# SyncE's transfers in the order as written, and a planner that expects later landings, in a two-layer encoder kernel

## The chip, the cores and the metric

The kernel runs on one NeuronCore of a Trainium2 chip. The core has five instruction queues that run side by side and wait for each other by semaphores: TensorE (PE, matrix products), VectorE (DVE), ScalarE (ACT), GpSimd (POOL) and SyncE (SP), which here does nothing but issue transfers (DMAs). The metric is the device time of one execution in microseconds (us); lower is better. All tensors are float32. Products use a split of each operand into a high and a low part (hi and lo) and three products (hi·hi, hi·lo, lo·hi), so every weight that is loaded has to pass ACT (hi) and POOL or DVE (lo = raw − hi) before PE can use it.

## The reference

Two layers of an encoder over 512 positions of width 1024 (a grid of 8 rows by 64 columns), and a last RMSNorm:

```
for l in range(DEPTH):                       # DEPTH = 2
    x = x + hybrid_mixer(rms_norm(x, norm_mix[l]), ...)      # one input projection, 8 neighbourhood heads
                                                             # and 8 grouped-query heads (2 k/v heads), w_out
    x = x + memory_cross_attention(rms_norm(x), rms_norm(mem), ...)   # 4 heads over 256 memory tokens
    x = x + conv_ffn(rms_norm(x), ...)       # up-projection to 2 x 2816, width-3 convolution over positions,
                                             # silu(gate) * val, down-projection
return rms_norm(x, norm_final)
```

Neighbourhood attention adds a learned bias to its scores and masks columns outside the window; the grouped-query heads normalise q and k per head and rotate them by a 2-D position table.

## The kernel before

The activations stay in SBUF transposed, as eight tiles xT of 128 features by 512 positions. The weights come through in pieces of at most 512 KB: SyncE loads a piece into one of two buffers (`raw`, `N_RAW = 2`), ACT writes the high part (`hi<-raw`, L709), POOL or DVE the low part (`lo<-raw,hi`, L710), and PE multiplies. A load into `raw` must wait until the low part of the piece before the last is written, as the buffer is free only then. A layer runs in this order: input projection in the order of `NA_ORDER` (q0, k0, q1, k1, v0 in two pieces, q2, k2, q3, k3, then four pieces `kv` and four `gq`), woven with the neighbourhood attention of four head pairs; grouped-query attention woven with the output projection and the memory keys and values; memory attention; the feed-forward block in three groups.

Beside the weights SyncE moves: biases (`r<-in_bias`, 2 x 384 KB for a head pair, L1076, used by `tensor_tensor_reduce` on the scores, L1264); parameters; memory tokens, once for their statistics (`t<-in_memT`, L1010, squared by ACT at L1012) and once as operands (L980); the rotary tables (L1334 and L1335, multiplied on POOL at L1337); and copies from SBUF to SBUF that bring rows to other partitions: `double` (L1154, `r<-r`, the two k tiles of a pair) and `straddle` (L1240, five copies, v at block borders).

The order on each engine isn't that of the text. The program is written once, and class `Order` then plans a new order for every engine. Each instruction is a `Step` with a duration from a small table. `lifetimes` and `due` work back from the products to a latest time for each step. `run` plays the program forward: on the engines in `FREE` it takes the step that is ready with the earliest latest time (`choose`), on PE it looks up to 240 products ahead for one whose operands are ready by `SURE` (600 ns) before (`product_next`). A transfer in that play costs `DMA_ISSUE` on SyncE, then lands `DMA_NS` later plus its bytes at `DMA_RATE` (330 bytes per ns, shared); at most eight are on the way (`DMA_MOST`). Sixteen rounds change the due times by the products that came late; each round's order is played twice with drawn latencies (`DMA_SPREAD`) and jitter, and the best order is kept. `tc.add_manual_dep` fixes it. SyncE is one of the engines in `FREE`: its transfers are ordered by need, apart from the first fifteen (`SP_IN_ORDER`).

The steps that the prediction speaks of, in the first layer's input projection (about 10 to 75 us):

- `split_k` and `split_q` (L1128 to L1165): a projection in PSUM is scaled by DVE (L1128, L1133), copied by ACT (L1144, L1163) and the rest subtracted by DVE (L1148, L1165). Only then is its PSUM bank (`mm`, four of them) free for the next product.
- `na_scores`: PE's scores, DVE adds the bias (L1264), ACT takes exponentials (L1270); `na_normalise` scales (L954 on POOL, L1282 on ACT); `na_transpose`: PE transposes (L1292), ACT and DVE split (L947, L948); `na_values`: PE multiplies by v (`mm<-r,r`), ACT and DVE combine (L1316 to L1318).

Of the kernel before, what the change touches and what calls it, by code (L numbers as in the profile page):

```python
# [19 lines left out]
P = 128  # L20
# [178 lines left out]
HAND_OVER = {"PE": 60.0, "ACT": 85.0, "DVE": 60.0, "POOL": 80.0, "SP": 60.0}  # L199
# [13 lines left out]
class Step:  # L213
# [99 lines left out]
class Order:  # L313
# [1 line left out]

    FREE = ("ACT", "DVE", "POOL", "SP")
    ORDERED = FREE + ("PE",)

    def __init__(self, tc, kept):
# [71 lines left out]
    def lifetimes(self):  # L393

        self.chain, self.then, self.previous = [list(v) for v in self.after], {}, {}
        first, users, turn = {}, {}, {}
        for s in self.steps:
            for name in s.names:
                if name not in first:
                    first[name] = s.index  # L400
                    turn.setdefault(s.kind(name), []).append(name)
                users.setdefault(name, []).append(s.index)
        for k in SLOTS:
            for old, new in zip(turn[k], turn[k][1:]):
                self.previous[new] = old
                self.then.setdefault(first[old], []).append(first[new])
        for k in IN_TURN:
            for old, new in zip(turn[k], turn[k][SLOTS[k]:]):
                for u in users[old]:
                    if u < first[new]:  # L410
                        self.chain[u].append(first[new])

    def due(self):

        start, now = {}, FIRST_PRODUCT
        for s in self.steps:
            if s.engine == "PE":
                start[s.index] = now - self.credit.get(s.index, 0.0)
                now += s.busy
        end = now + 1e4  # L420
        self.latest = [end] * len(self.steps)
        for s in reversed(self.steps):
            until = min([end] + [self.latest[j] - self.wait(s, self.steps[j]) for j in self.chain[s.index]])
            if s.engine == "PE":
                self.latest[s.index] = start[s.index]
            elif s.dma:
                self.latest[s.index] = until - DMA_NS - s.bytes / DMA_RATE
            else:
                self.latest[s.index] = min([until - s.takes] + [self.latest[j] for j in self.then.get(s.index, ())])

    def run(self, given=None, draw=None):


# [9 lines left out]
        written = [s.index for s in steps if s.engine == "PE"]  # L443
        at = 0
        open_ = {e: [s.index for s in steps if s.engine == e and not need[s.index]] for e in self.FREE}
        issued, shared = set(), {"DVE": 0.0, "POOL": 0.0}
        order, late, product = {e: [] for e in self.ORDERED}, [], None

        moving, clock, last, gate = [], 0.0, 0.0, 0.0

        def possible(j, ready):

            if need[j] or self.kept.get(j, -1) >= 0 and self.kept[j] not in issued:
                return None
            t, wanted = ready[j], {}
            if steps[j].engine == "SP":

                if len(moving) >= DMA_MOST:
                    return None
                t = max(t, gate)  # L460
# [12 lines left out]
            return t  # L473
# [34 lines left out]

        def product_next():

            mine, i, seen, best = written, at, 0, None
            while i < len(mine) and seen < AHEAD_MOST:
                j = mine[i]
                i += 1
                if j in issued:
                    continue
                seen += 1
                t = earliest(j)
                if t is None:
                    continue  # L520
                sure = max(t, possible(j, fed) + SURE)
                if best is None or sure < best[0] - PATIENCE:
                    best = sure, t, j
                if best[0] <= free_at["PE"] + PATIENCE:
                    break
            return best and best[1:]
# [44 lines left out]
        while len(issued) < n or moving:  # L571
            best = None
            for e in HAND_OVER:
                if e != "PE" or given is not None:
                    c = choose(e)
                else:
                    c = product_next()
                if c and c[0] is not None and (best is None or c[0] < best[0]):
                    best = c
            j = transfers(best[0] if best else 1e18)  # L580
            if j is not None:
                if len(moving) == DMA_MOST - 1:
                    gate = clock
                over_(steps[j], clock, clock)
                continue
            t, j = best
            s = steps[j]
            e = s.engine
            if e in self.FREE:
                open_[e].remove(j)  # L590
            if e in self.ORDERED:
                order[e].append(s)
            if e == "PE":
                short = MARGIN - (t - possible(j, fed))
                if product is not None and short > 0:
                    late.append((j, t - product, t - product + short))
                product = t + s.busy

            if e == "POOL":
                t = max(t, shared["DVE"])  # L600
                if s.wide(s.reads) or getattr(s.ins, "op", None) == ALU.pow:
                    shared["POOL"] = t + s.busy
            elif s.two_from_sbuf():
                t = max(t, shared["POOL"])
                shared["DVE"] = t + s.busy
            slow = 1.0 if draw is None or e in ("PE", "SP") else 1.0 + 0.04 * draw.random()
            free_at[e] = t + s.busy * slow
            issued.add(j)
            while at < len(written) and written[at] in issued:
                at += 1  # L610
# [17 lines left out]
def encoder_kernel(ctx: ExitStack, tc: tile.TileContext, t: dict, out: bass.AP):  # L628
    nc = tc.nc
    kept = set()  # L630
    PE, SP = Counted(nc.tensor), Free(nc.sync)
    SP_IN_ORDER = InOrder(tc, nc.sync, kept)
    late = Late(PE)
    ACT_IN_ORDER = InOrder(tc, nc.scalar, kept)
    ACT, DVE, POOL = Free(nc.scalar), Free(nc.vector), Free(nc.gpsimd)
# [191 lines left out]
    for n in FIRST:  # L827
        if isinstance(n, int):
            if n == 0:
                SP_IN_ORDER.dma_start(x0, t["x0"])  # L830
            else:
                SP_IN_ORDER.dma_start(xT[n], t["xT"][n * P : (n + 1) * P, :])
# [5 lines left out]
        (nc.scalar if n == FIRST[1] else SP_IN_ORDER).dma_start(raw[:, k0:k1], loads[0][1][:, k0:k1])  # L838
# [1066 lines left out]
```

## Time and profile before

| | |
|---|---|
| median of 3 runs | 1337.96 us (1336.49 to 1338.44) |
| the profiled execution's own time | 1337.63 us |
| its span in the profile | 1335.8 us |
| granted PE clock, mean of the span | 0.997 |
| transfers | 136.80 MB, 102 GB/s over the span |

The profile of one execution gives the busy time of each engine, the chain of waits that ended last, who waited for whom, and every instruction with its start. "Idle before" a group of instructions is the time in which the engine stood still, and the releaser behind the arrow is what ended it. A transfer has two times: its issue on SyncE's queue (SPq), and its landing, which is when its reader may start. The busy time of PE is modelled over pipelined products: one of 512 columns is listed with about 0.39 us while the next starts 0.23 us after it, so the gaps are better read from start times.

### The profile page before, as it was taken

Reading aid. Unit: us, or ns where it says so; the run is one execution under the profiler, and the core shown is the slowest. Engines: PE = TensorE matmul, PEld = TensorE weight load, DVE = VectorE, ACT = ScalarE, POOL = GpSimd, SP = SyncE. Lnnn points to the kernel's source line nnn. Section 1 sums busy time; section 2 is a strip of 40 time slices with the busy share of each in tenths; the row PEclk is TensorE's granted clock in tenths of the full one; section 3 lists DMA queues with packets and bytes.
Section 4 is the critical chain, followed back from the end, with each engine's and each line's share of the span. In section 5 each row is a group of like instructions: output and inputs, shape, how many; then the busy total and the mean of one; then the engine's idle time right before and its main releaser. Section 6 shows DMA issues by size and latency. Waiting matters only on the chain.

```text
span 1335.8 us, 18121 instructions
## 1 busy us (share of the span) xinstructions
PE 1326.2 (99%) x6544; PEld 1117.7 (84%) x6544; DVE 885.4 (66%) x1574; ACT 685.0 (51%) x1258; POOL 708.4 (53%) x496
## 2 busy tenths in 40 slices
PE   9999999999999999999999999999999999999998
PEld 8888888888888888888888888888888888888887
DVE  6569875675984388178535697776769825862874
ACT  6668776654442244244446687765544423432434
POOL 2667965636444443444736578664544444444443
PEclk9999999999999999999999999999999999999998
DMA  7753322313333333333356413222233333333321
GB/s 227 201 149 87 110 67 61 110 52 100 101 96 95 95 95 95 104 100 101 98 146 186 143 57 102 64 75 84 64 101 101 99 95 96 91 99 101 102 82 64
DMA packets 203706, 136.80 MB, mean 102 GB/s; under 512 B 5344, under 2 KB 193760, under 8 KB 203616
## 3 DMA queue, kind: packets, MB, share of 16 engines
q1 hardware_dynamic: 202800, 134.98, 34.7%
q8 instruction: 52, 0.85, 0.3%
q10 hardware_dynamic: 816, 0.66, 0.1%
q14 instruction: 38, 0.31, 0.1%
HBM read 125.65 MB, written 2.10 MB: 96 GB/s over the span
## 4 chain that ended last, share of the span: by engine, by line
PE 93%; ACT 2%; DVE 2%; DMA 1%; issue 1%; POOL 0%; SPq 0%; POOLq 0%; ACTq 0%; DVEq 0%
PE mm L95 81%; PE sc L95 7%; PE tr L1447 2%; PE tr L95 1%; PE tr L1292 1%; DMA r<-r 1%; PE tr L1626 1%; ACT t L1270 0%; ACT hi L709 0%; DMA raw<-in_w_in 0%; DVE r L1165 0%; ACT r L1144 0%; DVE sc L1264 0%; ACT r L947 0%; DVE r L948 0%
## 5 line engine op out<-in xcount | busy, mean ns | idle before, releaser
L710 POOL TENSOR_TENSOR lo<-raw,hi 128x512 fp32r<-128x512 f32 (+3 forms) x278 | 528.9, 1913 | 516.1 <-ACT hi L709 474.0
L95 PE MATMUL mm<-xg,hi 128*128 128x512 f32 x1728 | 534.1, 390 | 0.0
L709 ACT CAST hi<-raw 128x512 fp32r<-128x512 f32 (+3 forms) x282 | 232.1, 841 | 335.3 <-PE mm L95 277.1
L95 PEld LDWEIGHTS mm<-xg,hi 128*128 128x128 f32 x1728 | 322.6, 188 | 65.9
L95 PE MATMUL mm<-r,hi 128*128 128x512 f32 (+1 forms) x1200 | 348.7, 371 | 0.1
L95 PE MATMUL mm<-xg,lo 128*128 128x512 f32 x864 | 336.3, 389 | 0.0
L1728 DVE SCALAR_TENSOR_TENSOR t<-t,par,t 128x7 f32<-128x7 f32 (+1 forms) x352 | 245.9, 757 | 25.9 <-ACT t L1721 25.9
L95 PEld LDWEIGHTS mm<-r,hi 128*128 128x128 f32 x1200 | 217.9, 188 | 38.4 <-ACT hi L709 0.6
L95 PE MATMUL mm<-r,lo 128*128 128x512 f32 (+1 forms) x600 | 222.0, 371 | 0.0
L95 PEld LDWEIGHTS mm<-xg,lo 128*128 128x128 f32 x864 | 162.2, 188 | 33.8
L95 PEld LDWEIGHTS mm<-r,lo 128*128 128x128 f32 x600 | 113.0, 188 | 19.2
L95 PE MATMUL mm<-hi,xg 128*128 128x512 f32 (+1 forms) x384 | 110.4, 360 | 1.7 <-DVE r L1148 1.6
L1713 DVE TENSOR_TENSOR t<-mm,rep 128x512 f32<-128x512 f32 x88 | 60.0, 686 | 59.7 <-PE mm L95 44.0
L954 POOL TENSOR_SCALAR t<-t,s 128x512 f32<-128x512 f32 (+1 forms) x112 | 66.7, 611 | 57.7 <-DVE s L1431 33.7
L1757 DVE TENSOR_TENSOR xT<-xT,mm 128x512 f32<-128x512 f32 x32 | 21.9, 686 | 104.5 <-PE mm L95 104.5
L1733 ACT CAST r<-t 128x512 fp32r<-128x512 f32 x44 | 27.3, 620 | 108.9 <-DVE t L1731 108.9
L1731 DVE TENSOR_TENSOR t<-t,t 128x512 f32<-128x512 f32 x44 | 74.3, 1689 | 5.2 <-ACT t L1730 1.2
L95 PEld LDWEIGHTS mm<-hi,xg 128*128 128x128 f32 x384 | 68.1, 189 | 11.1 <-DVE r L1148 1.9
L95 PE MATMUL sc<-r,r 128*128 128x256 f32 (+1 forms) x352 | 74.3, 330 | 0.0
L95 PE MATMUL mm<-lo,xg 128*128 128x512 f32 (+1 forms) x192 | 68.4, 359 | 0.0
L1721 ACT ACTIVATE t<-t,par 128x512 f32<-128x512 f32 x88 | 67.0, 806 | 0.7 <-DVE t L1713 0.7
L1425 ACT ACTIVATE t<-sc,s,qr 128x512 f32<-128x512 f32 x64 | 49.3, 776 | 25.7 <-DVE s L954 25.1
(166 smaller groups left out, 1551.3 us busy)
## 6 DMA issues: line engine op xcount, KB each, us to landing
raw<-in_w_up SPq DMA_DIRECT2D x88, 512.0 KB, 3.8
raw<-in_w_in SPq DMA_DIRECT2D x25, 512.0 KB, 4.1
raw<-in_w_down SPq DMA_DIRECT2D x24, 448.0 KB, 3.6
raw<-in_w_down SPq DMA_DIRECT2D x20, 512.0 KB, 3.9
raw<-in_w_mem_kv SPq DMA_DIRECT2D x16, 512.0 KB, 3.8
r<-in_bias SPq DMA_DIRECT2D x16, 384.0 KB, 4.9
r<-r SPq DMA_DIRECT2D x22, 256.0 KB, 3.5
raw<-in_w_in SPq DMA_DIRECT2D x18, 256.0 KB, 3.9
```

The lines of the kernel that those rows point to most:

```text
L95: return self.engine.matmul(out, lhsT, rhs, **k)
L709: act.copy(hi[:, k], raw[:, k])
L710: (POOL if eng[0] == "P" else DVE).tensor_sub(lo[:, k], raw[:, k], f(hi)[:, k])
L954: eng.tensor_scalar(e, e, sums[:, col : col + 1], 1.0, op0=ALU.mult, op1=ALU.mult)
L1425: ACT.activation(e, sc[j], AF.Exp, bias=nmx[:, c], scale=qrs[b][:, col : col + 1], accum_out=sums[:, c])
L1447: PE.transpose(tr[:, k * P : (k + 1) * P], es[j][:, k * P : (k + 1) * P], ident)
L1713: DVE.tensor_mul(u, us[side], ffn.rep)
L1721: ACT.activation(cc, u, AF.Identity, bias=par[:, l, CB + ch : CB + ch + 1], scale=w[1])
L1728: DVE.scalar_tensor_tensor(cc[:, dst], u[:, src], wi, cc[:, dst], op0=ALU.mult, op1=ALU.add)
L1731: DVE.tensor_mul(cs[0], cs[0], cs[1])
L1733: ACT.copy(acts[j][0], cs[0])
L1757: DVE.tensor_add(xT[m], xT[m], pm)
```

## The change

Two sizes that the planner uses are moved, and one engine is taken out of its hands.

- `DMA_NS` goes from 3000 to 3500, `DMA_SPREAD` from 1900–3100 to 2700–4200, and `SURE` from 600 to 500.
- SyncE is no longer in `FREE`. All its transfers go through `InOrder`, in the order in which the program text issues them. The play takes them from a list (`written["SP"]`), and a transfer waits until the eighth before it in that list has landed (`gate`). The due time of a transfer is now no later than that of the next in the list (`queue`), and `lifetimes` makes a transfer also a forerunner of the one eight places behind it.
- In `possible`, a step may open a buffer only if it is the first in the text to use it.

```diff
-DMA_ISSUE, DMA_NS, DMA_RATE, DMA_SHARE, DMA_GAP, DMA_MOST = 480.0, 3000.0, 330.0, 0.6, 150.0, 8
+DMA_ISSUE, DMA_NS, DMA_RATE, DMA_SHARE, DMA_GAP, DMA_MOST = 480.0, 3500.0, 330.0, 0.6, 150.0, 8
-DMA_SPREAD, JITTER = (1900.0, 3100.0), 200.0
-AHEAD_MOST, PATIENCE, SURE = 240, 60.0, 600.0
+DMA_SPREAD, JITTER = (2700.0, 4200.0), 200.0
+AHEAD_MOST, PATIENCE, SURE = 240, 60.0, 500.0
...
-    FREE = ("ACT", "DVE", "POOL", "SP")
+    FREE = ("ACT", "DVE", "POOL")
...
+        queue = [s.index for s in self.steps if s.dma and s.engine == "SP"]
+        self.gate, self.follows = dict(zip(queue[DMA_MOST:], queue)), dict(zip(queue, queue[DMA_MOST:]))
+        for a, b in self.follows.items():
+            self.chain[a].append(b)
...
-                self.latest[s.index] = until - DMA_NS - s.bytes / DMA_RATE
+                queue = self.latest[s.index] = min(until - DMA_NS - s.bytes / DMA_RATE, queue - s.busy)
...
+            if j in self.gate and self.gate[j] not in landed:
+                return None
...
+                    if self.first[name] != j:
+                        return None
...
-    PE, SP = Counted(nc.tensor), Free(nc.sync)
-    SP_IN_ORDER = InOrder(tc, nc.sync, kept)
+    PE, SP = Counted(nc.tensor), InOrder(tc, nc.sync, kept)
```

No instruction is added or taken away: both programs have 323 transfers on SyncE and the same products. Only the places change. In the built programs 1102 of 6472 products, 291 of 1101 ACT instructions, 329 of 1574 on DVE, 86 of some 490 on POOL and 76 of 323 transfers have another place in their queue. All moved products lie, by their times in the profile before, between 23 and 300 us and between 729 and 954 us; in the feed-forward blocks PE's order is the same. The transfers that move most are those of the first 70 us. After the fifteen first loads SyncE's queue reads (weights by their names in `NA_ORDER`):

```
before: bias0, bias0, par, par, k1, gfin, v0a, memT1, v0b, q2, k2, double1, double1, q3, bias1, bias1,
        straddle x4, k3, straddle, memT2, rope, kv0 x2, qkg, kv1 x2, memT3, double2 x2, kv2 x2, bias2 x2, kv3 x2
after:  k1, v0a, v0b, q2, bias0, bias0, par, par, gfin, k2, q3, k3, double1, double1, memT1, bias1, bias1,
        straddle x5, kv0 x2, memT2, rope, qkg, kv1 x2, kv2 x2, memT3, double2 x2, bias2 x2, kv3 x2
```

On ACT the four exponentials of the second unit (L1270) stood behind the split of kv0 (L709) and now stand ahead of it; on POOL that unit's normalisation (L954) stood behind the low part of kv0 and the first half of the rotary table's product (L1337), and now stands ahead of both. At the end of the kernel two of the six result stores on SyncE change places.

More of the change, by code (lines that the diff above doesn't have):

```diff
@@ L395, in lifetimes @@
         self.chain, self.then, self.previous = [list(v) for v in self.after], {}, {}
-        first, users, turn = {}, {}, {}
+        self.first, users, turn = {}, {}, {}
+        first = self.first
         for s in self.steps:
@@ L420, in due @@
         end = now + 1e4
-        self.latest = [end] * len(self.steps)
+        self.latest, queue = [end] * len(self.steps), end
         for s in reversed(self.steps):
@@ L442, in run @@
                 left[name] = left.get(name, 0) + 1
-        written = [s.index for s in steps if s.engine == "PE"]
-        at = 0
+        written = {e: [s.index for s in steps if s.engine == e] for e in HAND_OVER}
+        at = dict.fromkeys(HAND_OVER, 0)
         open_ = {e: [s.index for s in steps if s.engine == e and not need[s.index]] for e in self.FREE}
-        issued, shared = set(), {"DVE": 0.0, "POOL": 0.0}
+        issued, landed, shared = set(), set(), {"DVE": 0.0, "POOL": 0.0}
         order, late, product = {e: [] for e in self.ORDERED}, [], None
-        moving, clock, last, gate = [], 0.0, 0.0, 0.0
+        moving, clock, last = [], 0.0, 0.0
         def possible(j, ready):
@@ L581, in run @@
             if j is not None:
-                if len(moving) == DMA_MOST - 1:
-                    gate = clock
+                landed.add(j)
+                if j in self.follows:
+                    ready[self.follows[j]] = max(ready[self.follows[j]], clock)
                 over_(steps[j], clock, clock)
@@ L605, in run @@
                 shared["DVE"] = t + s.busy
-            slow = 1.0 if draw is None or e in ("PE", "SP") else 1.0 + 0.04 * draw.random()
+            slow = 1.0 if draw is None or e not in self.FREE else 1.0 + 0.04 * draw.random()
             free_at[e] = t + s.busy * slow
             issued.add(j)
-            while at < len(written) and written[at] in issued:
-                at += 1
+            while e == "PE" and at[e] < len(written[e]) and written[e][at[e]] in issued:
+                at[e] += 1
             for name in s.names:
@@ L837, in encoder_kernel @@
         raw, loads = first_loads[u]
-        (nc.scalar if n == FIRST[1] else SP_IN_ORDER).dma_start(raw[:, k0:k1], loads[0][1][:, k0:k1])
+        (nc.scalar if n == FIRST[1] else SP).dma_start(raw[:, k0:k1], loads[0][1][:, k0:k1])
     ACT_IN_ORDER.copy(small(1), ones)
```

21 lines of the change are left out of this document (12 added, 9 removed).

## The prediction

> **What bounds the kernel now.** I read the page's head first, then who waited for whom on PE, then the windows, then the chain of waits in the one stretch where PE stood still. The page says that PE is the bound:
>
> ```profile
> span 1335.8 us, 18121 instructions
> PE 1326.2 (99%) x6544; PEld 1117.7 (84%) x6544; DVE 885.4 (66%) x1574; ACT 685.0 (51%) x1258; POOL 708.4 (53%) x496
> ...
> raw<-in_w_up SPq DMA_DIRECT2D x88, 512.0 KB, 3.8
> ```
>
> PE is idle for 1335.8 − 1326.2 = 9.6 us, start and end included. The change adds no product and takes none away, so it can win only part of these 9.6 us, while nothing caps what it may lose. The waits of PE (engine, line, releaser, us in total, times, longest) are:
>
> ```profile
> PE mm L95 <- DVE r L1148: 1.6, 1, 1.6
> PE tr L95 <- POOL ident masks.py:199: 1.3, 1, 1.3
> PE mm L95 <- DVE t L1318: 0.3, 1, 0.3
> PE tr L95 <- POOL s L940: 0.3, 1, 0.3
> ```
>
> The second and fourth stand at the start and in the tail, which keep their order. One wait in the body is worth anything: a product that wanted a PSUM bank until DVE had emptied it. By stretch (busy us of PE, PEld, DVE, ACT, POOL, granted clock, DMA share, GB/s):
>
> ```profile
> 10.00:21.00 11.00, 11.00 (x50) 9.09 (x50) 9.61 (x14) 10.20 (x19) 1.23 (x1) 1.00 0.97 302
> 39.00:44.00 5.00, 5.00 (x33) 4.51 (x33) 1.89 (x4) 1.25 (x4) 3.76 (x4) 1.00 0.72 181
> 44.00:57.00 13.00, 13.00 (x67) 11.04 (x66) 6.13 (x21) 6.29 (x17) 6.58 (x8) 1.00 0.89 220
> 57.00:72.00 15.00, 14.46 (x80) 12.22 (x78) 7.60 (x18) 12.15 (x31) 13.88 (x13) 1.00 0.70 211
> ...
> 400.00:450.00 50.00, 50.00 (x223) 41.39 (x222) 17.60 (x22) 12.76 (x15) 23.17 (x10) 1.00 0.34 95
> ...
> 750.00:800.00 50.00, 49.54 (x277) 41.52 (x276) 43.65 (x106) 41.06 (x101) 40.66 (x43) 1.00 0.36 111
> 800.00:850.00 50.00, 49.88 (x257) 41.12 (x256) 36.73 (x82) 36.55 (x78) 38.74 (x40) 1.00 0.33 95
> ```
>
> The feed-forward blocks (400 to 450 stands for them) have no idle PE and keep their order; their transfers are hidden at a DMA share of 0.34. What can change lies in the first layer's projection and in the same place of the second (0.46 + 0.12 us idle between 750 and 850). The chain of waits behind the 1.6 us (start, us, what):
>
> ```profile
> 41.45 8.90 DMA r<-r
> ...
> 50.83 5.85 DMA raw<-in_w_in
> ...
> 56.78 1.15 ACT hi L709 x2
> ...
> 59.15 1.94 ACT t L1270 x8
> ...
> 71.64 0.68 DVE r L1148
> 72.36 0.71 DVE r L1148
> ...
> 73.11 2.11 PE mm L95 x8
> ```
>
> The straddle copies took 8.90 us to land in a full DMA system; the eight-in-flight limit held kv0's load until then; ACT stood at kv0's split until 56.78 with the second unit's exponentials (L1270) queued behind it; the delay went through ACT and DVE to the emptying of a bank at 72.36 + 0.71 = 73.07, and PE went on at 73.11.
>
> **The change part by part.**
>
> *SyncE's first transfers.* k1 and v0a now go ahead of two biases, the parameters and a memory tile, in a stretch with share 0.97: they land earlier, PE has no gap there, gain 0. The biases wait instead behind v0b and q2, 16 us later than before; their first reader is past 44 us, so cost 0. The price is paid later: `double1`, memT1, bias1 and the straddles stand behind k3, whose load waits for the low part of k2. From the time lines of POOL, SyncE and ACT:
>
> ```profile
> 40.41 2.54 POOL L710 TENSOR_TENSOR lo<-raw,hi 128x512 fp32r<-128x512 f32 x2
> ...
> 35.57 1.24 SPq L1154 DMA_DIRECT2D r<-r  x2
> ...
> 39.43 1.98 SPq L1076 DMA_DIRECT2D r<-in_bias  x2
> ...
> 61.20 1.54 SPq L696 DMA_DIRECT2D raw<-in_w_in  x2
> ...
> 53.63 1.14 ACT L709 CAST hi<-raw 128x512 fp32r<-128x512 f32 x2 [3.55 <-DMA raw<-in_w_in]
> ...
> 56.78 1.15 ACT L709 CAST hi<-raw 128x512 fp32r<-128x512 f32 x2 [1.47 <-DMA raw<-in_w_in]
> ...
> 61.74 1.12 ACT L709 CAST hi<-raw 128x512 fp32r<-128x512 f32 x2
> ```
>
> That low part ends at 40.41 + 2.54 = 42.95, so k3 is issued at about 43.0, `double1` some 8 us later than its 35.57, the biases some 6 us later. From 43.0 the queue moves, in MB: k3 0.52, double1 0.52, memT1 0.26, bias1 0.79, straddles 0.79, kv0 0.52 (3.41 in all), memT2 0.26 (3.67), rope and qkg 0.33 (4.00), kv1 0.52 (4.52). A lone 512 KB load lands 3.8 us after issue, of which 0.52 MB at 302 GB/s is 1.7, so bytes flow from about 43.0 + 2.1 = 45.1. At 302 GB/s kv0 lands at 56.4 and kv1 at 60.1; at 247 (the 220 of the row for 44 to 57, which has the same mix of copies and loads, over its share of 0.89) at 58.9 and 63.4. At 220 flat they land at 60.6 and 65.6. Before, they were there at 56.78 and 61.74 at the latest, so this edit alone makes kv0 and kv1 later by up to 4 us, and earlier by nothing that counts.
>
> *ACT's and POOL's new order.* k3 has little ahead of it, lands at about 47.7 and is split 5 us before its 53.63. After it the second unit's exponentials are next and no longer wait for kv0. When their bias additions ended is read from a gap in DVE's time line; with it stand rows of ACT and PE:
>
> ```profile
> 59.16 1.41 DVE L1148 TENSOR_TENSOR r<-mm,r 64x512 fp32r<-64x512 f32 x2 [3.62 <-ACT r L1144]
> ...
> 71.64 1.41 DVE L1148 TENSOR_TENSOR r<-mm,r 64x512 fp32r<-64x512 f32 x2 [2.67 <-ACT r L1144]
> ...
> 63.25 0.58 ACT L947 CAST r<-tr 128x512 fp32r<-128x512 f32 x1
> ...
> 66.72 1.11 PE L95 MATMUL mm<-r,r 128*128 128x256 f32 x8
> ...
> 73.11 0.50 PE L95 MATMUL mm<-hi,xg 128*128 128x512 f32 x1 [1.65 <-DVE r L1148]
> ```
>
> (59.16 − 3.62 = 55.54: DVE had nothing to do from there, which is when the additions were over.) So the exponentials run from about 55.5 to 57.5 instead of 59.15 to 61.09: 4 us are won on ACT. POOL scales that unit by about 59, then takes kv0's low part (2.5 us as for k2), so kv2's load, which waits for that, is issued at about 61.5, as before (61.20).
>
> Now ACT's queue: kv0's split, memT2's square, the first half of kv1's split, two L1144, one L1163, then the L947 of the first unit's transposed scores, which PE multiplies by v at 66.72. From the start of kv1's half to the start of that L947 are 0.52 + 0.59 + 0.59 + 0.60 = 2.3 us, then 0.58, and 0.69 on DVE (L948); the second L947 with its L948 ends 1.3 us after the first. With kv1 at 60.1 they are done at 63.7 and 65.0; at 63.4, at 67.0 and 68.3. PE wants the first at 66.72, the second half a us later (67.2): no stall at 302 GB/s, 1.1 at 247, and 3.3 at 220. The bank of the 1.65 us: kv2 lands at about 66.5 (61.5 plus the 3.8 to 5.85 of the rows above), then one half split, two L1144 and the two L1148 (1.41): 66.5 + 0.6 + 1.2 + 1.41 = 69.7, with 71.6 for the 5.85 and a late DVE. PE wanted it at 73.11 − 1.65 = 71.46. So this gap closes: −1.65, with an open end of +0.2. Between the two rates I take a new stall of 0.5, nearer to none since memT2, rope and the later loads are partly interleaved with the copies: the stage gives −1.65 + 0.2 + 0.5 = −0.95, bounds −1.65 and +1.65.
>
> [...]
>
> *PE's own order.* 1102 products move, in 23 to 300 and 729 to 954 us. I held the new place of each (start times of before, summed along the new order) against the times at which its inputs were ready in the trace. Eight products come too early, by 0.25 to 0.67 us each and 4.0 us in all; the first and the one in the second layer:
>
> ```profile
> 118.36 0.69 DVE L1148 TENSOR_TENSOR r<-tr,r 64x512 fp32r<-64x512 f32 x1
> ...
> 788.56 5.05 POOL L710 TENSOR_TENSOR lo<-raw,hi 128x512 fp32r<-128x512 f32 x4
> ...
> 791.16 0.50 PE L95 MATMUL mm<-lo,r 128*128 128x512 f32 x1
> ```
>
> The transposes that wanted this DVE result at 119.21 now want it at 118.4, while it ends at 119.05. The product of the second half of a low part, started at 791.16 when POOL's second of four was done (788.56 + 2.5), is now wanted at 790.45. Cost: 4.0 us if every input comes as before, 0 or less if ACT's and DVE's own new order (291 and 329 moved) brings them sooner. Of the four largest, three wait for a result behind an ACT copy that has moved forward by two to six places; the fourth, the one at 791, waits for a POOL step that hasn't moved. I take +0.3, bounds −0.6 (the idle of 750 to 850 gone) and +4.0.
>
> *The rest.* The straddles of pair 1 in the first layer come 5 us later, behind the first memory-key piece, but their products are late enough by over a us: 0. The biases of layer 2 go from 630 to 662 us, used past 700: 0. Two of the stores change places at the end; the last two stores follow them and their data is later still: 0. The planner's sizes cost nothing by themselves.
>
> Sum: −0.95 + 0.3 = −0.65 against the profiled execution's 1337.63, which gives 1337.0. That execution is 0.33 below the median of the runs (1337.96), so I predict 1337.0, about 0.05% below before.
>
> **The rivals.**
>
> *Slower: kv1 lands late, and ACT waits for it with the first unit's split scores behind it.* One place, 60 to 68 us. The second L948 ends 4.9 us after kv1's landing (65.0 after 60.1), so each us by which kv1 lands after 62.3 is a us of PE past 67.2. The gain of 1.45 is eaten at 63.7, and without the +0.3 from elsewhere 0.2% (2.7 us) is lost when kv1 lands past 66.4, which is 4.52 MB in 21.3 us, 212 GB/s. The row for 57 to 72 has 211, and that for 39 to 44 has 181: at 200 GB/s kv1 lands at 67.7 and the time is 1337.63 + 5.4 − 1.45 + 0.3 = 1341.9. Against it: those two stretches had shares of 0.70 and 0.72, so they weren't full. [...]
>
> *Slower by small stalls.* The eight early products cost their 4.0 us, perhaps more with the lower reserve of 500 ns: 1337.63 − 0.95 + 4.0 = 1340.7. For it: DVE and ACT are busy over 80% of the time where the last of them lie (43.65 and 41.06 of 50 us). Against it: PE's idle in before was 0.58 there, with the same planner.
>
> *Faster by over 0.2%.* The gap of 1.65, the 0.58 of the second layer and half a us of small gaps all go: 1337.63 − 2.7 = 1334.9. That is nearly all the body has to give.
>
> *The change doesn't reach PE.* The order of transfers is hidden anyway, and the 1.65 us only moves to 67 us: 1337.6 to 1338.0.
>
> **How the numbers follow.** 0.2% or 2.7 us is about what a measurement of this kernel can tell from no change; the three runs spread over 1.95 us. Forecast 0.42, and with it the change that doesn't reach PE 0.10, both within. Late kv1 0.23, of which 0.18 is beyond 0.2%. Small stalls 0.12, of which 0.08 is beyond. Faster 0.13, of which 0.12 is beyond. Within: 0.42 + 0.10 + 0.05 + 0.04 + 0.01 = 0.62; slower 0.26; faster 0.12. The range goes from 1334.9 (the body's idle gone) to 1341.5, nearly the late kv1 at 200 GB/s; outside lie about 0.06 below and 0.12 above.
>
> **What would show it.** In the profile after: the exponentials of the second unit ahead of kv0's split on ACT, starting near 55 us; no wait of PE on L1148 at 71 us; kv1's split between 60 and 63.5 us, and a wait of PE on L948 near 67 us of at most 1 us; PE's waits in 110 to 140 and 780 to 800 us below 1 us each. I am wrong if PE's idle time is above 13 us or below 7, and wrong in the mechanism if the wait on L1148 stays.

## The result, and the profile after

The changed kernel takes 1340.84 us (median of 10 runs, 1339.27 to 1341.96), the kernel before beside it 1337.80 us (median of 10): a ratio of 1.0022, 95% interval 1.0015 to 1.0030, or 2.0 to 4.0 us slower. I had predicted 1337.0 us. The profiled execution of the changed kernel took 1339.94 us with a span of 1338.2 us, 2.4 us above the 1335.8 before.

The page of the changed kernel, its head:

```profile
span 1338.2 us, 18123 instructions
PE 1326.0 (99%) x6544; PEld 1116.6 (83%) x6544; DVE 894.8 (67%) x1574; ACT 684.4 (51%) x1258; POOL 708.2 (53%) x496
```

PE has the same work (1326.0 us against 1326.2) and 12.2 us of idle time instead of 9.6. The waits of PE after (engine, line, releaser, us in total, times, longest; from about line 700 on, a line of before has moved down by 12, so L1148 is L1160 now, L1165 is L1177, L997 is L1009, L1395 is L1407):

```profile
PE tr L95 <- POOL ident masks.py:199: 1.3, 1, 1.3
PE tr L1459 <- DVE r L1177: 1.3, 2, 0.9
PE mm L95 <- POOL lo L722: 1.2, 2, 0.6
PE mm L95 <- DVE t L1330: 0.7, 1, 0.7
PE tr L1374 <- DVE r L960: 0.3, 1, 0.3
```

The wait of 1.6 us on L1148 is gone, as predicted. The view has nine lines where before had four; five of them stand here. By stretch (the windows, columns as in the prediction), the changed kernel:

```profile
44.00:57.00 13.00, 13.00 (x64) 10.93 (x64) 6.30 (x22) 7.34 (x23) 6.15 (x8) 1.00 1.03 271
57.00:72.00 15.00, 15.00 (x82) 12.76 (x81) 8.59 (x19) 10.89 (x25) 12.53 (x12) 1.00 0.80 242
72.00:100.00 28.00, 27.40 (x149) 23.39 (x149) 17.67 (x57) 19.82 (x55) 16.91 (x20) 1.00 0.47 139
100.00:150.00 50.00, 48.97 (x273) 41.42 (x272) 43.44 (x101) 39.40 (x95) 40.27 (x42) 1.00 0.37 107
750.00:800.00 50.00, 49.27 (x272) 40.91 (x271) 43.90 (x102) 38.93 (x97) 39.40 (x42) 1.00 0.38 112
800.00:850.00 50.00, 48.13 (x244) 38.94 (x243) 37.46 (x81) 37.24 (x81) 39.58 (x40) 1.00 0.32 95
```

and the two of before that the prediction did not show:

```profile
72.00:100.00 28.00, 26.89 (x147) 23.30 (x148) 17.55 (x54) 18.59 (x52) 15.67 (x19) 1.00 0.52 151
100.00:150.00 50.00, 49.98 (x278) 42.23 (x277) 46.13 (x105) 39.88 (x97) 40.03 (x41) 1.00 0.35 100
```

Length less busy PE gives the balance. From 57 to 100 us the idle time falls from 0.54 + 1.11 = 1.65 us to 0.60: 1.05 us won. From 100 to 150 us it rises from 0.02 to 1.03, and from 750 to 850 us from 0.46 + 0.12 = 0.58 to 0.73 + 1.87 = 2.60: 1.01 and 2.02 us lost. Together 1.98 of the 2.4 us. Most of the rest lies behind the last product, 6.2 us after and 5.7 before; `early` below, which ends on the old lists, has 6.2 too, so this is scatter between executions. So the part that I argued at length came out, and the part to which I gave 0.3 us decided. The single gaps, from the time line of PE (in brackets the idle time before the instruction and its releaser):

```profile
77.09 0.50 PE L95 MATMUL mm<-lo,xg 128*128 128x512 f32 x1 [0.60 <-POOL lo L722]
...
123.73 0.66 PE L1374 MATMUL tr<-ident,t 128*128 128x128 f32 x4 [0.32 <-DVE r L960]
...
135.96 0.71 PE L95 MATMUL mm<-r,r 128*128 128x256 f32 x4 [0.70 <-DVE t L1330]
...
806.22 0.63 PE L1459 MATMUL tr<-ident,t 128*128 128x128 f32 x4 [0.94 <-DVE r L1177]
...
807.19 0.63 PE L1459 MATMUL tr<-ident,t 128*128 128x128 f32 x4 [0.34 <-DVE r L1177]
...
810.57 0.50 PE L95 MATMUL mm<-r,lo 128*128 128x512 f32 x1 [0.55 <-POOL lo L722]
```

The largest group, at 806 to 811 us, waits for DVE, or for POOL, which waits for DVE in turn. Its time line there, in the changed kernel:

```profile
795.25 0.99 DVE L1009 SCALAR_TENSOR_TENSOR r<-r,par,r 128x256 fp32r<-128x256 f32 x1
796.17 1.25 DVE L1407 TENSOR_SCALAR s<-s,geps 128x8 f32<-128x8 f32 x1
...
799.66 0.48 DVE L1009 SCALAR_TENSOR_TENSOR r<-r,par,r 128x256 fp32r<-128x256 f32 x1
...
800.96 1.60 DVE L1009 SCALAR_TENSOR_TENSOR r<-r,par,r 128x256 fp32r<-128x256 f32 x1
...
804.68 1.39 DVE L1177 TENSOR_TENSOR r<-tr,r 64x512 fp32r<-64x512 f32 x2
```

before:

```profile
793.73 0.85 DVE L997 SCALAR_TENSOR_TENSOR r<-r,par,r 128x256 fp32r<-128x256 f32 x1
795.06 0.23 DVE L1395 TENSOR_SCALAR s<-s,geps 128x8 f32<-128x8 f32 x1
...
798.83 0.63 DVE L997 SCALAR_TENSOR_TENSOR r<-r,par,r 128x256 fp32r<-128x256 f32 x1
...
801.00 0.69 DVE L1165 TENSOR_TENSOR r<-tr,r 64x512 fp32r<-64x512 f32 x1
```

and POOL in the changed kernel:

```profile
794.68 1.29 POOL L986 TENSOR_TENSOR r<-t,r 128x512 fp32r<-128x512 f32 x1
795.99 2.65 POOL L722 TENSOR_TENSOR lo<-raw,hi 128x512 fp32r<-128x512 f32 x2
800.98 2.72 POOL L722 TENSOR_TENSOR lo<-raw,hi 128x512 fp32r<-128x512 f32 x2 [2.34 <-ACT hi L721]
```

Three DVE steps take 0.99, 1.25 and 1.60 us where they took 0.85, 0.23 and 0.63: 2.1 us longer together. The two long ones start within 0.2 us of a POOL step and end within 0.3 us of that step's end (each POOL row holds two steps, of which the first is meant: 796.17 + 1.25 = 797.42 against 795.99 + 1.40 = 797.39; 800.96 + 1.60 = 802.56 against 800.98 + 1.29 = 802.27), and the same L1009 step takes 0.48 us at 799.66, when POOL is idle. The second subtraction of the first unit (L1165, now L1177) ended at 801.7; now it ends at 806.1 and PE goes on at 806.2. Of these 4.4 us the three long steps are 2.1; 1.4 are two steps that now stand ahead of this subtraction and stood behind it; by the remaining 0.9 us DVE was late already.

These rows are of the second layer. They don't explain the 1.01 us of the first: from 100 to 150 us DVE is less busy than before (43.44 us against 46.13), and before has a 128x8 step of 1.30 us there too (L1395 at 138.12), without a stall of PE. What makes that part was not found; a long DVE step by itself doesn't make a stall.

### The profile page after: what moved, and what is told of

It is laid out like the page before. It is cut to its first block, busy times and chain, and to the rows that moved or that the text cites. A ratio compares the mean times of both kernels' runs of the same rounds, so it can differ in the third digit from the quotient of the medians.

```text
span 1338.2 us, 18123 instructions
## 1 busy us (share of the span) xinstructions
PE 1326.0 (99%) x6544; PEld 1116.6 (83%) x6544; DVE 894.8 (67%) x1574; ACT 684.4 (51%) x1258; POOL 708.2 (53%) x496
## 4 chain that ended last, share of the span: by engine, by line
PE 90%; DVE 3%; ACT 3%; DMA 1%; POOL 1%; issue 1%; POOLq 0%; SPq 0%; ACTq 0%; DVEq 0%
PE mm L95 79%; PE sc L95 7%; PE tr L1459 2%; PE tr L95 1%; DMA r<-r 1%; POOL lo L722 1%; PE tr L1638 1%; ACT r L1156 0%; PE tr L1304 0%; DVE r L1009 0%; ACT r L959 0%; ACT t L1282 0%; DVE r L1177 0%; DVE t L1330 0%; DVE r L960 0%
## 5 line engine op out<-in xcount | busy, mean ns | idle before, releaser
L722 POOL TENSOR_TENSOR lo<-raw,hi 128x512 fp32r<-128x512 f32 (+3 forms) x278 | 529.4, 1914 | 518.0 <-ACT hi L721 480.0
L1740 DVE SCALAR_TENSOR_TENSOR t<-t,par,t 128x7 f32<-128x7 f32 (+1 forms) x352 | 251.2, 772 | 26.4 <-ACT t L1733 26.4
L966 POOL TENSOR_SCALAR t<-t,s 128x512 f32<-128x512 f32 (+1 forms) x112 | 66.3, 604 | 55.9 <-DVE s L1443 31.7
```

The costliest lines, as they stand in the source:

```text
L722: (POOL if eng[0] == "P" else DVE).tensor_sub(lo[:, k], raw[:, k], f(hi)[:, k])
L966: eng.tensor_scalar(e, e, sums[:, col : col + 1], 1.0, op0=ALU.mult, op1=ALU.mult)
L1740: DVE.scalar_tensor_tensor(cc[:, dst], u[:, src], wi, cc[:, dst], op0=ALU.mult, op1=ALU.add)
```

## The experiments

Two theories at the start. **A:** the loss is small stalls in the dense stretches after 100 us, and the first transfers are not to blame. **B:** the transfers that land later cost it through what queues behind them. The first three kernels work out both plans and cut each engine's list where both have issued the same instructions (code in outline, names shortened):

```
+    was, now = Was(tc, kept), Now(tc, kept | sp_names)       # the two planners, each with its sizes
+    for e in was.plan:
+        steps, done = [], 0
+        for which, until in was.step_at(parts):              # early: [("now", 77.0), ("was", None)]
+            end = len(was.plan[e]) if until is None else cut_at(...)
+            steps += (now if which == "now" else was).plan[e][done:end]
+            done = end
```

**The changed plan up to 77 us alone (`early`).**

> All engines and SyncE take the changed plan up to 77 us and the old plan from there on (both plans are worked out, and each engine's list is cut where the two have issued the same instructions). Theory A (the loss lies in small stalls after 100 us, where DVE and ACT are dense, and has nothing to do with the first transfers): PE loses the old gap of 1.65 us at 71 us, keeps the 0.76 us at 76 us that the changed kernel shows, and nothing else moves: about 1 us faster than before, 1336.8 us. Rival B (the transfers that land later in 45 to 70 us cost it, through the buffers and engines behind them): the loss of the changed kernel stays, 1340 to 1341 us. Rival C (any new list shifts the whole of what follows by chance): anywhere in 1336 to 1341, with stalls at places after 100 us that neither kernel shows.

Measured 1335.96 us against 1336.90, ratio 0.9993 (0.9984 to 1.0002). Its windows:

```profile
57.00:72.00 15.00, 15.00 (x83) 12.88 (x83) 8.62 (x19) 11.14 (x27) 12.71 (x12) 1.00 0.81 241
72.00:100.00 28.00, 27.65 (x151) 23.64 (x150) 17.54 (x57) 19.85 (x56) 16.94 (x20) 1.00 0.55 159
```

0.35 us idle where before has 1.65, and 0.57 after 100 us (table below), as in before. B falls: with the changed order of the first transfers there is no loss. C's stalls at new places didn't come either. The median is the lowest of all kernels here; the interval doesn't separate it from before.

**The two layers apart (`layer1`: changed plan up to 500 us; `layer2`: from 500 us).**

> The changed plan up to 500 us (the whole first layer's mixer), the old plan from there on. Theory A: 1.05 us won at 57 to 100 us and 1.0 us lost at 100 to 150 us cancel, and the second layer is as before: 1337.5 to 1338.2 us, no difference. Rival B (late first transfers are the whole loss): 1340 to 1341 us. Stalls in 788 to 811 us must be those of before (0.6 us) by A.

> The old plan up to 500 us, the changed plan from there on. Theory A: the second layer's new stalls, 2 us of idle PE between 788 and 811 us, and some tenths at the end: 1339.8 to 1340.8 us, most of the loss. Rival B (first transfers): 1337.8, no difference. If layer1 and layer2 together give the loss of the whole change, the two layers are independent, and the cause of each can be sought by itself.

Measured: `layer1` 1337.29 us, 1.0001 (0.9992 to 1.0010); `layer2` 1340.55 us, 1.0027 (1.0017 to 1.0038), all of the loss. Windows of `layer2`:

```profile
57.00:72.00 15.00, 14.34 (x79) 12.11 (x77) 8.53 (x19) 12.18 (x32) 13.12 (x14) 1.00 0.69 214
72.00:100.00 28.00, 27.86 (x151) 24.08 (x152) 17.53 (x58) 18.15 (x50) 15.49 (x19) 1.00 0.53 155
...
800.00:850.00 50.00, 48.13 (x244) 39.12 (x244) 37.47 (x81) 37.29 (x80) 39.64 (x40) 1.00 0.32 92
```

PE's busy time in 800 to 850 us is that of the changed kernel to a hundredth: these stalls belong to the lists. The gap at 71 us does not. This kernel runs the old lists there, and has 0.66 + 0.14 = 0.80 us idle where the profile of before had 1.65.

**Whose list (`others2`: from 500 us the changed lists, but PE's old one; code in outline).**

```
-            steps += (now if which == "now" else was).plan[e][done:end]
+            steps += (now if which == "now" and e != "PE" else was).plan[e][done:end]
```

> The old plan up to 500 us; from there PE keeps its old list and ACT, DVE, POOL and SyncE take the changed ones. Theory P (the loss of the second layer comes from PE's own new list, which wants products earlier, as the prediction's step 'PE's own order' has it): the stalls go, 1337 to 1338 us. Theory D (DVE is 2 us late at 797 to 803 us, since three of its steps ran beside POOL steps and took 2.1 us longer, and so the last L1177 subtractions end 3 to 4 us later; PE's list matters little): the stalls before the L1447 transposes near 805 us stay, 1339 to 1340.5 us.

Measured 1341.87 us, 1.0036 (1.0023 to 1.0048). PE (lines stand 360 further down here: L1326 is the L966 of the changed kernel):

```profile
806.58 0.50 PE L95 MATMUL sc<-r,r 128*128 128x512 f32 x1 [1.69 <-DVE s L1326]
810.78 0.63 PE L1819 MATMUL tr<-ident,t 128*128 128x128 f32 x4 [0.98 <-DVE s L1326]
```

Theory P falls: with the old places of PE's products the stalls don't go, they are worse, 1.4 us above the upper end of what D had said. So PE's new list isn't needed for them; the new lists of the other engines are enough. That PE's new list had been made to fit the other new lists would explain why they are worse, but isn't shown. The counterpart, PE's new list with the old ones of the others, was not run.

**One DVE step moved (`away1`, `ahead`).** The first moves the 1.60 us step into the time when POOL is idle, the second restores the old place of the subtraction that PE waits for (instructions described, not by their names in the program):

```
+MOVES = [("DVE", second L1009 step of the tile, ahead of the L1330 pair)]             # away1
+MOVES = [("DVE", second L1177 of the first unit, ahead of the second L1434)]          # ahead
```

> The changed kernel with one DVE step moved: the second L1009 step of a tile in the second layer (1.60 us beside a POOL step that starts in the same instant at 801 us) goes two places forward, to 800.1 us, where POOL has nothing to do. Nothing else moves. Theory D (that step's 1 us is part of DVE's lateness): it takes about 0.5 us, the steps behind it end 1.1 us sooner, and PE's idle time near 805 to 811 us falls by 1 to 1.7 us: 1339.1 to 1339.9 us. Rival (the lateness comes from the order of the L1177 subtractions behind the reductions of the next unit, or PE waits for something else): the time stays within 0.4 us of the changed kernel's 1340.8 us.

> The changed kernel with another single DVE step moved: the second L1177 subtraction of the first unit (805.4 us, for which PE waits 1.1 us at 804.9 us) goes ahead of the second reduction of s (L1434) and of the next unit's subtraction, two places, as the old plan had it. Theory D (DVE is late as a whole): the first wait goes, but the steps put behind it end 0.7 us later, so the second wait grows by as much: 0.4 us won at most, 1340.3 to 1341 us. Rival O (the order of these subtractions is the cause): 1.1 us won, 1339.7 us.

Measured: `away1` 1338.97 us, 1.0017 (1.0008 to 1.0026); `ahead` 1340.46 us, 1.0026 (1.0017 to 1.0035). Neither interval is clear of the changed kernel's; the verdict is from the traces. Lines stand 6 further down in these two. `away1`, its DVE (two steps in one row), PE and window:

```profile
799.57 0.88 DVE L1015 SCALAR_TENSOR_TENSOR r<-r,par,r 128x256 fp32r<-128x256 f32 x2
```

```profile
805.86 0.63 PE L1465 MATMUL tr<-ident,t 128*128 128x128 f32 x4 [0.24 <-DVE r L1183]
...
809.24 0.50 PE L95 MATMUL mm<-r,lo 128*128 128x512 f32 x1 [0.54 <-POOL lo L728]
```

```profile
800.00:850.00 50.00, 49.18 (x250) 40.06 (x249) 37.51 (x84) 37.92 (x82) 39.38 (x40) 1.00 0.31 94
```

The step now takes 0.48 us, the waits before the transposes fall from 0.94 + 0.34 to 0.24, and the idle time of the stretch from 1.87 to 0.82 us: D by 1.05 us, the low end of what it said. In `ahead` the idle time is 2.40 us, since what was put behind came later (DVE's last subtraction ends at 808.42, POOL's L1414, which the view names, at 808.44):

```profile
808.57 0.63 PE L1465 MATMUL tr<-ident,t 128*128 128x128 f32 x4 [1.60 <-POOL qr L1414]
```

So for the largest group the mechanism is shown in part: DVE as a whole is late, and one step beside POOL makes 1.05 of the 1.75 us that this stretch gained in idle time (1.87 less 0.12 before). Putting the one subtraction back in its old place doesn't help. The share of the 1.25 us step was not tried.

**Which edit (`order_only`, `sure_back`, `dma_back`, `sizes_alone`).** The sizes put back in the changed kernel, all or in part, and the sizes put into the kernel before:

```
-DMA_NS = 3500.0;  DMA_SPREAD = (2700.0, 4200.0);  SURE = 500.0
+DMA_NS = 3000.0;  DMA_SPREAD = (1900.0, 3100.0);  SURE = 600.0     # order_only
+DMA_NS = 3500.0;  DMA_SPREAD = (2700.0, 4200.0);  SURE = 600.0     # sure_back
+DMA_NS = 3000.0;  DMA_SPREAD = (1900.0, 3100.0);  SURE = 500.0     # dma_back
```

> The new planner with SyncE in the order as written, but with the old sizes (landing 3000 ns, drawn from 1900 to 3100 ns, reserve 600 ns). SyncE's lists are those of the changed kernel. If the written order is the cause: 1340 to 1341 us. If the sizes are (a product is taken with 500 ns in reserve instead of 600, and 1116 products stand elsewhere than in the changed kernel): the gain at 71 us stays and the stalls after 100 us go, about 1336.8 us. If both plans are only different draws of the same planner: in between, with stalls of its own.

> The changed kernel with the reserve for a product put back to 600 ns; the new landing time and spread and SyncE's written order stay. If the thinner reserve is what lets PE meet inputs that are a little late (the stalls of 118 to 135 and 789 to 811 us): those stalls go, about 1337 us. If the landing sizes are: 1340 to 1341 us. If each setting only draws another plan: a time between, with stalls at other places.

> The changed kernel with landing time and spread put back (3000 ns, 1900 to 3100 ns); the reserve of 500 ns and SyncE's written order stay. If the thinner reserve is the cause: 1340 to 1341 us, with stalls in the dense stretches of both layers. If the landing sizes are: about 1337 us. With the run beside it this splits the sizes in two.

> The kernel before with the three new sizes and SyncE's transfers still ordered by the planner (with the one line of the change that lets only a tile's first step take its slot, without which the list of transfers locks up). If the longer landing time by itself spoils the lists of DVE and POOL (Theory L): stalls of PE in 100 to 150 us or 785 to 812 us, 1339 to 1342 us. If the loss needs the written order of the transfers too: 1336.5 to 1338 us.

Measured: `order_only` 1337.02 us, 1.0002 (0.9994 to 1.0011); `sure_back` 1341.80 us, 1.0037 (1.0024 to 1.0049); `dma_back` 1338.30 us, 1.0011 (1.0002 to 1.0020); `sizes_alone` 1340.61 us, 1.0024 (1.0015 to 1.0033). Two guesses fell: the reserve of 500 ns, which I had blamed, is not it (with 600 the kernel is no faster), and the written order with the old sizes costs no time in `order_only`. That time is the one guessed, but not for the guessed reason: the stalls after 100 us didn't go, PE is idle there for 1.89 us against 0.60 before (table below), and the 1.65 us won from 57 to 100 us pays for them. Of these four lists, those planned with the longer landing are the slower ones, with either order of the transfers.

**Is it the size, or the draw? (`land2250`, `draw1`, `draw2`, `old_draw1`, `old_draw2`, `before_seed1`)** Theory L: the planned landing is further from the real one (5.1 us for 512 KB against medians of 3.4 to 4.0 by weight in the changed kernel's trace, 750 to 850 us), so a shorter one must do better. Rival N: each setting is another draw of lists that scatter.

```
+DMA_NS = 2250.0;  DMA_SPREAD = (1650.0, 2850.0);  SURE = 600.0     # land2250
+SEED = 1;  e, _, more = self.run(order, random.Random(i + 7))      # draw1; 2 and 20 in draw2
+... and order_only's sizes                                         # old_draw1, old_draw2
+SEED = 1                                                           # before_seed1, in before
```

> The changed kernel with a landing time of 2250 ns (drawn from 1650 to 2850 ns) and the reserve at 600 ns. With the planner's rate of 330 bytes a ns a 512 KB load then lands 3.8 us after its issue, as the trace shows (3.4 to 4.2 us in 750 to 850 us); with 3000 it lands after 4.6 us, with 3500 after 5.1 us. Theory L (the further the planned landing is from the real one, the worse the lists fit): no new stalls over 1 us, 1335.5 to 1337.5 us. Rival N (each size is only another draw): anywhere between 1336 and 1342 us.

> The changed kernel with other random draws (another seed for the credits, other seeds for the replays), the same sizes. 87 PE and 65 DVE places of the second layer differ from the changed kernel's. If the loss belongs to the sizes: 1340 to 1342 us again, with stalls in 788 to 812 us. If it is chance of one draw: it may be gone, 1337 to 1339 us.

> The changed kernel with a third set of draws; its PE list of the second layer is that of the changed kernel, with 11 DVE and 14 ACT places otherwise. Whatever the cause, the second layer's PE stalls in 788 to 811 us should be those of the changed kernel (2.6 us idle), unless these few places move DVE away from POOL: 1339.5 to 1341 us.

> The new planner with SyncE's written order and the old sizes, as in the run of the order alone (1337.0 us), with other random draws; 347 PE places of the second layer differ from that run's. Scatter (the old list and that run's are good draws): 1338 to 1341 us, with stalls of 2 to 4 us in 100 to 150 and 750 to 850 us together. Sizes (the old sizes give good lists): 1336.5 to 1337.7 us.

> The same with a third set of draws. Scatter: 1338 to 1341 us. Sizes: 1336.5 to 1337.7 us.

> The kernel before with another seed for the credits, nothing else; 118 PE places differ, 66 of them in the second layer. Scatter: slower than before by 0.5 to 3 us, with stalls in the second layer that before does not have. Sizes: no difference, 1336.5 to 1337.7 us.

Measured: `land2250` 1340.89 us, 1.0030 (1.0018 to 1.0041); `draw1` 1338.23 us, 1.0010 (1.0002 to 1.0019); `draw2` 1340.32 us, 1.0024 (1.0015 to 1.0033); `old_draw1` 1338.54 us, 1.0012 (1.0003 to 1.0021); `old_draw2` 1338.00 us, 1.0010 (1.0001 to 1.0019); `before_seed1` 1336.56 us, 0.9998 (0.9989 to 1.0007). L falls: `land2250` has DVE and POOL collide in the first layer. Its DVE, its POOL and its PE:

```profile
142.78 1.60 DVE L1009 SCALAR_TENSOR_TENSOR r<-r,par,r 128x256 fp32r<-128x256 f32 x1
```

```profile
142.80 2.73 POOL L722 TENSOR_TENSOR lo<-raw,hi 128x512 fp32r<-128x512 f32 x2 [1.29 <-ACT hi L721]
```

```profile
149.26 0.50 PE L95 MATMUL sc<-r,r 128*128 128x512 f32 x1 [2.56 <-ACT t L1437]
```

And `draw1`, with the changed kernel's sizes, is out of step with POOL by a quarter of a us, its L1407 starting just ahead of POOL's step and not just behind it:

```profile
796.33 0.22 DVE L1407 TENSOR_SCALAR s<-s,geps 128x8 f32<-128x8 f32 x1
...
800.01 0.88 DVE L1009 SCALAR_TENSOR_TENSOR r<-r,par,r 128x256 fp32r<-128x256 f32 x2
```

```profile
796.37 2.58 POOL L722 TENSOR_TENSOR lo<-raw,hi 128x512 fp32r<-128x512 f32 x2 [0.25 <-ACT hi L721]
```

All the kernels in one table: idle PE by stretch (length less busy, from the windows), the duration of two of the DVE steps above, which lie at 793 to 805 us (us, from the traces), and the ratio.

| kernel | 57–100 | 100–200 | 750–800 | 800–850 | L1407 | second L1009 | ratio |
|---|---|---|---|---|---|---|---|
| before | 1.65 | 0.02 | 0.46 | 0.12 | 0.23 | 0.63 | 1 |
| before_seed1 | 1.97 | 0.02 | 0.41 | 0.17 | 0.23 | 0.64 | 0.9998 |
| early | 0.35 | 0.02 | 0.41 | 0.14 | 0.23 | 0.62 | 0.9993 |
| layer1 | 0.27 | 1.10 | 0.45 | 0.15 | 0.23 | 0.64 | 1.0001 |
| order_only | 0.00 | 0.04 | 1.45 | 0.40 | 1.25 | 0.83 | 1.0002 |
| draw1 | 0.11 | 0.94 | 0.52 | 0.43 | 0.22 | 0.48 | 1.0010 |
| old_draw2 | 0.00 | 0.04 | 1.37 | 1.03 | 0.22 | 0.95 | 1.0010 |
| dma_back | 0.26 | 0.15 | 1.67 | 0.59 | 1.25 | 0.83 | 1.0011 |
| old_draw1 | 0.00 | 0.03 | 1.43 | 1.78 | 1.25 | 1.61 | 1.0012 |
| away1 | 0.62 | 1.11 | 0.77 | 0.82 | 1.25 | 0.48 | 1.0017 |
| **after** | 0.60 | 1.03 | 0.73 | 1.87 | 1.25 | 1.60 | 1.0022 |
| sizes_alone | 0.00 | 1.97 | 1.08 | 0.46 | 0.22 | 1.51 | 1.0024 |
| draw2 | 0.73 | 0.89 | 0.52 | 2.19 | 1.25 | 1.60 | 1.0024 |
| ahead | 0.61 | 1.10 | 0.52 | 2.40 | 1.25 | 1.61 | 1.0026 |
| layer2 | 0.80 | 0.02 | 0.74 | 1.87 | 1.25 | 1.60 | 1.0027 |
| land2250 | 0.73 | 2.87 | 0.97 | 0.01 | 0.23 | 0.63 | 1.0030 |
| others2 | 0.10 | 0.04 | 1.55 | 2.74 | 1.26 | 1.60 | 1.0036 |
| sure_back | 0.27 | 2.90 | 0.82 | 0.84 | 0.22 | 0.97 | 1.0037 |

The three stretches from 100 us on add up to 0.57 to 0.60 us in before, `before_seed1` and `early`, and to 1.7 to 4.6 in every other list. Six of the seven lists whose second L1009 step took 1.5 us or more have over 1.7 us idle in 800 to 850; `sizes_alone` is the exception. These are not seven draws: five of them (after, `ahead`, `layer2`, `others2` and `draw2`) have nearly the same DVE list there. The 1.25 us step alone goes with little idle time in 800 to 850 (0.40 in `order_only`, 0.59 in `dma_back`), yet both lists idle for over 1.4 us in 750 to 800, by waits that were not followed up.

What is shown: the loss is a matter of which list comes out, the same list stalls at the same places each time, and the written order of the transfers doesn't stall PE directly. Both rivals are half right. Draws scatter: `draw1` loses 0.10% where the changed kernel loses 0.22%, with the same sizes; their intervals overlap (1.0002 to 1.0019, 1.0015 to 1.0030), but the idle time of the four stretches is 2.00 us against 4.23. `old_draw1` and `old_draw2` also came out as scatter had said.

But `before_seed1` was no slower than before, against what scatter alone said, and the four lists with written order and a landing of 3000 ns lose 0.02 to 0.12%, where five planned with 3500 ns (both orders) lose 0.10 to 0.37% and the one with 2250 ns loses 0.30%. The two ranges touch. The table shows where they differ: from 100 to 200 us every list drawn up with 3000 ns has 0.02 to 0.15 us of idle PE, and every one drawn up with 3500 or 2250 ns has 0.89 to 2.90; from 750 to 850 us the sizes make no such difference (1.85 to 3.21 with the written order and 3000 ns, 0.95 to 2.71 with 3500). Why the first layer is quieter with 3000 ns stays open.

## Why the prediction was wrong, point by point

**The first transfers, right.** The order as written does what I worked out. `double1` is issued at 43.2 us, right behind k3 (42.74, and I had 43.0), where I had some 8 us after 35.57:

```profile
43.20 1.18 SPq L72 DMA_DIRECT2D r<-r  x2
```

and ACT follows (the second unit's exponentials, kv0's split, the first half of kv1's):

```profile
54.58 0.47 ACT L1282 ACTIVATE t<-sc,s 128x256 f32<-128x256 f32 x1 [3.27 <-DVE s L1276]
...
57.82 1.14 ACT L721 CAST hi<-raw 128x512 fp32r<-128x512 f32 x2 [0.55 <-POOL t L966]
...
60.88 0.62 ACT L721 CAST hi<-raw 128x512 fp32r<-128x512 f32 x1 [1.39 <-DMA raw<-in_w_in]
```

I had said 55.5 us for the exponentials; they start at 54.58. I had said kv1 at 60.1 us for 302 GB/s; it was split at 60.88, as soon as it was there. That is 4.52 MB in 60.9 − 45.1 = 15.8 us, 286 GB/s, nearer to my upper rate than to the lower, and the window of 44 to 57 us shows 271 at a full DMA share (1.03). So kv1 was hardly later than before (split by 61.74 at the latest), the wait on L948 near 67 us did not come, and the rival of a late kv1 fell.

**The stage's −0.95 us, right in size, in part by luck.** The profile gives −1.05. Its parts differ: no 0.5 us at 67, but 0.60 at 77, where PE waits for a low part on POOL. And I took the 1.65 us at 71 us as a property of the old kernel. It was one execution's: with the same lists up to 500 us the stretch has 0.80 and 0.10 us in `layer2` and `others2`; the chain in the prediction ties it to the landing of kv0. What there was to win on average was less; `early` puts it at 0.9 us, with an interval from 2.1 to below nothing.

**PE's own order, +0.3 us, the step that failed.** It measured +3.0 us (1.01 + 2.02), and so the forecast of −0.8 us against the 1337.80 measured beside it became a loss of 3.0. Its upper bound of 4.0 held, and the rival built on it, small stalls at 1340.7 us, gives the time that came (1340.84); I gave it 0.12. That the number fits is luck, as the largest waits are not at its eight products. Three things were wrong in the step.

- I held PE's new places against the times at which the old lists had the inputs ready. Inputs are made by DVE, ACT and POOL, whose lists were new too. Of the eight places that I had found too early, 118 to 119 and 791 us show no wait; the largest stalls, at 806 us, weren't among them. `others2` shows that in the second layer the stalls come without PE's new list.
- I kept the durations of before. Three DVE steps took 2.1 us longer beside POOL, in a stretch where DVE is busy for 43.9 of 50 us and has little time to catch up. The first layer's 1.01 us is not explained by this.
- "PE's idle in before was 0.58 there, with the same planner" was no evidence for a quiet new list. With the first layer's dense stretch before has 0.60; the lists planned anew have 1.9 to 4.6, but for `before_seed1`, which is closest to the old list.

**The rest.** Biases, straddles and stores cost nothing, as said: PE has no wait there, and 0 to 44 us has 1.34 us of idle PE against 1.35. I wrote that I'd be wrong if PE's idle time went above 13 us; it is 12.2, so that sign was set too wide for an effect of 3 us.

## What to carry to other kernels

When a change makes a planner draw up new lists, the old list's idle time in the dense stretches says little of the new one's: here it was 0.6 us, and 1.7 to 4.6 in nearly all the others. Other draws of the planner, made before the forecast, would have shown the size of that term. Hold new places against what the new lists make ready, not the old; and see whether a step of one engine has been moved beside a step of another with which it takes longer, as the 128x256 step here took 1.60 us beside POOL's and 0.48 without. A gap that hangs on a transfer's landing belongs to one execution until a second one shows it: the 1.65 us here were 0.80 and 0.10 in two others with the same lists.

## What the runs showed of the hardware

A DVE step of 128x8 elements (L1407), 0.22 us with POOL idle (changed kernel, 138.22 us), takes 1.25 us when it starts 0.2 us behind a POOL step (L722), and ends 0.03 us after it; started 0.04 us ahead of one it takes 0.22 (`draw1`). A scalar_tensor_tensor on 128x256 (L1009) takes 0.48 us with POOL idle (799.66 us) and up to 1.60 beside such a step: it ends 0.28 us behind the POOL step's end, and did so in before (0.85 us at 793.73, 0.63 at 798.83) as it does after (0.99 at 795.25, 1.60 at 800.96). So the old lists meet POOL too, there for a shorter time. It isn't so beside every POOL step: beside one of 128x8 elements (L1408) it took 0.48 us (changed kernel, 142.14 us). In these rows the long DVE step ends 0.03 to 0.29 us behind POOL's; why, no trace shows. The order of the starts, as listed, doesn't tell which step is long: of two that start ahead of POOL's, the 128x8 step 0.04 us ahead took its usual 0.22 us and the 128x256 step 0.02 us ahead took 1.60. The planner's code lets only DVE steps with two operands of over 16 elements wait for POOL and prices the 128x8 step at 0.12 us, so it couldn't see the 1.25; whether this is why its lists collide there was not tried. All of DVE is 9.4 us busier than before for the same 1574 instructions, most of it off PE's path. The clock didn't fall in any of these gaps: it was granted at 1.00 through the 2.56 us at 147 us in `land2250` as well. In before and in the changed kernel it falls only at the end, to 0.50, between 1328 and 1329 us in before and between 1333 and 1334 us in the changed kernel; why it comes there was not followed up.
